# A hybrid attention and convolution layer: turning the normed latents, and spreading the input's row norm, by VectorE and DRAM in place of TensorE

## The chip, the core and the metric

The kernel runs on one core of a Trainium2 chip. The core has TensorE (matmuls, with a separate weight load for each, results in PSUM), VectorE, ScalarE, GpSimd (called POOL in the profile) and SyncE (SP), which here only issues transfers; sixteen DMA engines move data between DRAM and SBUF for all the queues. In the profile VectorE is DVE and ScalarE is ACT. The metric is the device time of one execution in microseconds, as a median over runs.

## The reference, cut to what matters

The layer takes `x` (256 tokens by 2048 features) in float32, normalises its rows, and projects it with one wide `w_in` to ten pieces. The change touches the path of the first three pieces: the query latent, the key-value latent (512 features each) and the rotary key (64).

```python
def _rmsnorm(x, g):
    r = lax.rsqrt(jnp.mean(xf * xf, axis=-1, keepdims=True) + RMS_EPS)
    return (xf * r * g).astype(x.dtype)

h = _rmsnorm(x, pre_norm_g)
proj = jnp.einsum('bsd,de->bse', h, w_in)
(q_a, c_kv, k_rope, z_mla, c_in, b_gate, c_gate, z_conv, g_mla, g_conv) = jnp.split(proj, cuts, axis=-1)
q  = jnp.einsum('bsr,re->bse', _rmsnorm(q_a, q_a_norm_g), w_q_b)
kv = jnp.einsum('bsr,re->bse', _rmsnorm(c_kv, kv_a_norm_g), w_kv_b)
...
k_rope = _apply_rope(k_rope, cos, sin)
attn = _causal_mla_attention(q_nope, q_rope, k_nope, k_rope, v)
attn = attn * jax.nn.silu(z_mla)
...
x = x + _rmsnorm(out, post_norm_g)
```

Sixteen heads of attention follow, a gated short convolution beside it, two output projections with sigmoid gates, and one more projection with a norm.

## The kernel before, in words

**Precision.** Each float32 operand of a large matmul is kept as a high part and a low part, both in the fp32r type, and a product is three matmuls: high by high, high by low, low by high (`product`, L221). The high part is a copy on ScalarE and the low part a subtraction on VectorE (`split_act`, L236, for the weights; the same two engines with a scale for `x`, in `split_scaled`, L334).

**Layout.** `x_both` holds `x` with features on the partitions, times the norm's gain. The row factor of the input's norm is not applied to it: it is a number per token, `r_col` (tokens on partitions) or `r_x` (a row of 256 that stands on all partitions), and it multiplies results later.

**Weights.** All weight pieces stand in one list (`plan`, L106), in the order in which TensorE uses them: the query latent's pieces (these carry `x` too), the key-value latent's four, the rotary key's, then per head the gate's, the group's and the convolution's. `load_raw` (L150) issues them on SP's queue into three `raw` buffers; `split_unit` (L162) splits each half of a piece into `whi` and `wlo`, of which there are five each. `ahead` (L196) is called at each use and traces loads up to three pieces ahead and splits one piece ahead. A load waits until the splits of the piece three before it are done; a split waits until TensorE has finished the half that had its slot.

**Order.** The program is traced in the order of the code, and a planner that simulates the core's timeline then chooses the order on each engine among what is ready. `keep_in_program_order` pins an instruction behind the last one traced before it on its engine. Matmuls are pinned, and so are the transfers of `turned` on GpSimd's queue and the table work on GpSimd; weight loads, weight splits and most other work are not. On each engine and queue the chosen order is then kept: an instruction that waits holds up those behind it.

**The stage of the change.** The loops at L495 and L501 compute the two latents with tokens on partitions (`latent_products`, L456). After the second `ckv` piece the input's row norm is computed (`input_norm`, L361) and the query latent is normed (`latent_norm`, L465): squares on ScalarE, a power on GpSimd, a scaled copy from PSUM to `lat_f` in SBUF. The rotary key `kr` follows (L514), then `input_rows` (L374): two float32 matmuls of a matrix of ones with the diagonal matrices `dg` put the row factors on all partitions, and ScalarE copies them to `r_x`. Then the key-value latent is normed.

The next products need the latents with features on the partitions. `latent_turn` (L477) does that with eight TensorE transposes against the identity `ident` for each latent, into two PSUM banks, and from there ScalarE and VectorE make the high and low parts in `qa` and `ckv` with the norm's gain as the scale. It is called in the first gate (`gates`, L663; `z` in the profile): for `qa` after its first quarter, for `ckv` inside its second. Then come `key_rope` (L523) after the third quarter, `gates_done` (L668: sigmoid on ScalarE, product on VectorE), and the first head's groups: `qn` and `kn` (L545), `qr` (L554) and `vv` (L567), then the convolution's products `cv` and the scores `sc` (L582).

Elsewhere the kernel turns blocks another way: `turned` (L308) transposes 32x32 blocks on VectorE into a buffer `via`, stores it to a DRAM tile `far` with four transfers that put the blocks in their places, and loads it back. It is used on GpSimd's queue for the probabilities, gates and channels.

Of the kernel before, what the change touches and what calls it, by code (L numbers as in the profile page):

```python
# [10 lines left out]

F32 = mybir.dt.float32
F32R = mybir.dt.float32r
# [5 lines left out]
P = 128  # L19
S = 256  # L20
# [62 lines left out]
def tile_layer(ctx: ExitStack, tc: tile.TileContext, xw, x, pos, pvec, post_g, wc, wz, wcv, wkr, wqk, wqr, wv, cwr, wsq, out):  # L83
    nc = tc.nc

    def matmul(*a, **kw):

        return tc.keep_in_program_order(nc.tensor.matmul(*a, **kw))  # L88

    def transpose(*a):  # L90
        return tc.keep_in_program_order(nc.tensor.transpose(*a))  # L91

    const = ctx.enter_context(tc.tile_pool(name="const", bufs=1))
    top = ctx.enter_context(tc.tile_pool(name="top", bufs=1, side="right"))
# [156 lines left out]
        o, _ = PV[name]  # L251
        return pv[:, o + k : o + k + 1]

    ident = const.tile([P, P], F32, name="ident")
    make_identity(nc, ident[:, :])
    ones = const.tile([P, P], F32, name="ones")
    nc.gpsimd.memset(ones[:, :], 1.0)
    mhalf = const.tile([P, 1], F32, name="mhalf")
# [5 lines left out]
    idle = bank("idle", tag="st", bufs=1)  # L264
    for _ in range(9):
        matmul(idle[:, :P], ones[:, :], ones[:, :], start=True, stop=True)
    const.tile([P, LINE - 8 + 112], F32, name="const_pad")
    cos_t = const.tile([P, S], F32, name="cos_t")
    sin_t = const.tile([P, S], F32, name="sin_t")
    r_x = const.tile([P, S], F32, name="r_x")  # L270
# [29 lines left out]
    def temp(name, shape=(P, S), dt=F32, bufs=2, tag=None):  # L300

        tag, n = tag or name.rstrip("0123456789_"), shape[-1]
        if n % LINE == 0:
            return bp.tile(list(shape), dt, name=name, tag=tag, bufs=bufs)
        return bp.tile([P, -(-n // LINE) * LINE], dt, name=name, tag=tag, bufs=bufs)[:, :n]


    def turned(src, via, n):  # L308

        via = via[:, : P * n]  # L310
        v = via.rearrange("p (q k x) -> p q k x", q=4, k=n)
        nc.vector.transpose(v.rearrange("p q k x -> p k q x"), src)  # L312
        far = dram.tile([P, P * n], F32, name="far", tag=f"far{n}", bufs=4)

        def go():
            f = far[:, :].rearrange("(q y) (i m) -> i y q m", q=4, i=4)
            for i in range(4):
                m = via[32 * i : 32 * i + 32, :].rearrange("y (q m) -> y q m", q=4)
                tc.keep_in_program_order(nc.gpsimd.dma_start(out=f[i], in_=m))  # L319

        def come(dst):

            tc.keep_in_program_order(nc.gpsimd.dma_start(out=dst, in_=far[:, :]))

        return go, come

# [34 lines left out]
    def input_norm():  # L361
        ss = squares("x", [(x_tok[:, t, :], x_tok[:, t, :]) for t in range(NT)])
        v = temp("v_x", (P, NT), tag="rms_v")
        nc.vector.tensor_scalar(v[:, :], ss[:, :], 1.0 / D, EPS, op0=ALU.mult, op1=ALU.add)
        inverse_root(r_col[:, :], v[:, :])
        nc.vector.tensor_tensor(r_sq[:, :], r_col[:, :], r_col[:, :], op=ALU.mult)
        dgs = []
        for t in range(NT):
            dg = temp(f"dg{t}", (P, P), tag=f"rms_d{t}", bufs=1)
            nc.vector.tensor_scalar(dg[:, :], ident[:, :], r_col[:, t : t + 1], None, op0=ALU.mult)  # L370
            dgs.append(dg)
        return dgs

    def input_rows(dgs):  # L374

        rb = bank("rb", tag="st", bufs=1)
        for t in range(NT):
            matmul(rb[:, t * P : (t + 1) * P], ones[:, :], dgs[t][:, :], start=True, stop=True)
        nc.scalar.activation(r_x[:, :], rb[:, :S], AF.Copy)


    def whole(dst, ps):
# [82 lines left out]
    def latent_norm(name, pss):  # L465

        f = lat_f[name]
        ss = squares(name, [(pss[t][:, :], f[:, t, :]) for t in range(NT)])
        v, r = temp(f"v_{name}", (P, NT), tag="rms_v"), temp(f"r_{name}", (P, NT), tag="rms_r")
        nc.vector.scalar_tensor_tensor(v[:, :], ss[:, :], 1.0 / R, r_sq[:, :], op0=ALU.mult, op1=ALU.mult)  # L470
        nc.vector.tensor_scalar(v[:, :], v[:, :], EPS, None, op0=ALU.add)
        inverse_root(r[:, :], v[:, :])
        nc.vector.tensor_tensor(r[:, :], r[:, :], r_col[:, :], op=ALU.mult)
        for t in range(NT):
            nc.scalar.activation(f[:, t, :], pss[t][:, :], AF.Copy, scale=r[:, t : t + 1])

    def latent_turn(name, both, g, tags):  # L477
        f = lat_f[name]
        for j2 in range(2):
            ps = bank(f"lt_{name}{j2}", tag=tags[j2][0], bufs=tags[j2][1])  # L480
            for j in range(2):
                for t in range(NT):
                    o, b = j * S + t * P, 2 * j2 + j
                    transpose(ps[:, o : o + P], f[:, t, b * P : (b + 1) * P], ident[:, :])
            for j in range(2):
                b, src = 2 * j2 + j, ps[:, j * S : (j + 1) * S]
                nc.scalar.activation(both[:, b, :S], src, AF.Copy, scale=col(g, b))
                nc.vector.scalar_tensor_tensor(
                    both[:, b, S:], src, col(g, b), both[:, b, :S].bitcast(F32), op0=ALU.mult, op1=ALU.subtract
                )  # L490

    table_parts = tables()
    next(table_parts)
# [7 lines left out]
    for i in range(4):  # L501
        w = take(u_ckv[i])
        for k4 in range(4):
            latent_products(ps_c, 4 * i + k4, w, k4)
        if i == 0:
            next(table_parts)
        if i == 1:
            dg = input_norm()
            latent_norm("qa", ps_q)
            next(table_parts)  # L510
    ahead(u_kr)
    w = splits.pop(u_kr)
    ps = bank("kr")
    for k in range(KD):  # L514
        matmul(ps[:, :], w[k // 8][:, k % 8], x_both[:, k, :], start=k == 0, stop=k == KD - 1)
    input_rows(dg)
    latent_norm("ckv", ps_c)
    whole(kr_f, ps)
    nc.vector.tensor_copy(kr_g[:DR, :], kr_f[DR:, :])
    nc.vector.tensor_copy(kr_g[DR:, :], kr_f[:DR, :])  # L520
# [129 lines left out]
    at_t = at_f[:, :, :].rearrange("p (v t k) s -> p v t (k s)", v=NV, t=NT)  # L650
    z_ps = {}

    def quarter(pss, w, i, between=None):

        for t in range(NT):
            if t and between:
                between()
            for k4 in range(4):
                k = 4 * i + k4
                a = [x_both[:, k, o + t * P : o + (t + 1) * P] for o in (0, S)]  # L660
                product(pss[t][:, :], a, w(k4, 512), k == 0, k == KD - 1)

    def gates(v, i, between=None):  # L663
        if i == 0:
            z_ps["now"] = [bank(f"z{v}_{t}") for t in range(NT)]
        quarter(z_ps["now"], take(u_gate[v][i]), i, between)

    def gates_done(v):  # L668
        for t in range(NT):
# [92 lines left out]
    for h in range(H):  # L762
        v, at = divmod(h, HV)

        if at == 0:
            for i in range(4):
                if v == 0 and i == 1:

                    def turn_keys():
                        latent_turn("ckv", ckv, "kv_g", (("mm", 4), ("mm", 4)))  # L770
                        next(table_parts)

                    gates(v, i, turn_keys)
                else:
                    gates(v, i)
                if v == 0 and i == 0:
                    latent_turn("qa", qa, "q_g", (("st", 1), ("o", 1)))
                elif v == 0 and i == 2:
                    key_rope()
                elif v and i == 0:  # L780
                    arrive()
                elif v and i == 1:
                    pt = turn(ps_by_head.pop(h - 1))
                    next(tap)
                elif v and i == 2:
                    values(h - 1, pt)
                    make("v", v)
            if v:
                next(tap)
            gates_done(v)  # L790
        if h == 0:
            for i in first:
                make(*i)
            channels(h, 0)
        if h < H - 1:
            score(h)
        if h:
            channels(h, 0)
        if at == 0:
            coming.append(gates_turn(v, 0))  # L800
        channels(h, 1)
        if at == 0:
            arrive()
            coming.append(gates_turn(v, 1))
        else:
            pt = turn(ps_by_head.pop(h - 1))
        if h == H - 2:
            score(h + 1)

        if at == 2 or h == H - 1:  # L810
            next(tap)
        if at and h < H - 1:
            arrive()
        channels(h, 2)
        if at:
            values(h - 1, pt)
        else:
            arrive()
            if v:
                coming.append(channels_join(v - 1, 0))  # L820
        for i in made[h]:
            make(*i)
        if h == H - 1:
            pt = turn(ps_by_head.pop(h))
        channels(h, 3)
        if at == 2 or h == H - 1:
            next(tap)
        while coming and h < H - 1:
            arrive()
        if h == H - 1:  # L830
            values(h, pt)
        if at == 3:
            coming.append(channels_join(v, 1))
        if at == 1:
            tap = taps(v, 1)
            next(tap)
        elif at == 3 and h + 1 < H or h == H - 2:
            tap = taps(v, 0)
            next(tap)
# [244 lines left out]
```

## Time and profile before

| | |
|---|---|
| median of 3 runs | 1038.01 us (1038.0 to 1038.07) |
| the profiled execution | 1039.19 us, its span 1037.4 us |
| TensorE busy | 1027.2 us, 99% of the span |
| VectorE, ScalarE, GpSimd busy | 682.3, 526.6, 181.0 us |
| transfers | 231.04 MB, mean 223 GB/s |
| granted TensorE clock | 0.998 |

All times below are in microseconds from the start of the span unless marked ns. A row of a timeline has the start, the length, the engine, the line of the kernel, the operation, and the tiles as output<-inputs with their shapes; in brackets stands how long the engine stood idle before it and what ended that. A "q" behind an engine's name means its instruction queue, where transfers are issued. Matmuls are pipelined: their records overlap, so a row's length is not what an instruction adds to the time.

### The profile page before, as it was taken

To read this page: it belongs to the slowest core of one execution; us is meant where nothing else is said; L and a number is where in the kernel's file an instruction comes from. 1 tells how busy PE (TensorE), PEld (TensorE's weight loads), DVE (VectorE), ACT (ScalarE), POOL (GpSimd) and SP (SyncE) were. 2 spreads that over 40 slices of the span, in tenths; PEclk is the share of its full clock that TensorE was granted. 3 is DMA by queue.
4 is the path that set the end of the run, shared out by engine and by line. 5 is a ranking of instruction groups with operands and counts; after the bars stand their busy time and mean duration, and the time that the engine had idled before them with its cause. 6 is when DMAs were issued, how large, how long until landed. Compare 5 with 4: busy or idle time off the path is not lost.

```text
span 1037.4 us, 12723 instructions
## 1 busy us (share of the span) xinstructions
PE 1027.2 (99%) x4694; PEld 856.3 (83%) x4694; DVE 682.3 (66%) x954; ACT 526.6 (51%) x733; POOL 181.0 (17%) x345
## 2 busy tenths in 40 slices
PE   9999999999999999999999999999999999999996
PEld 7888888888888888888888888888888888888885
DVE  7579777787687786767777785564465455455562
ACT  7767555555555455554554564444334434443551
POOL 7620321114211232212313120020010001002000
PEclk9999999999999999999999999999999999999999
DMA  8745766568565685757676766565555566558642
GB/s 323 304 175 215 232 213 234 193 222 295 190 250 202 219 282 189 272 210 243 236 262 200 261 228 212 183 228 198 203 203 209 197 203 236 181 191 331 235 165 82
DMA packets 41952, 231.04 MB, mean 223 GB/s; under 512 B 7521, under 2 KB 8225, under 8 KB 18977
## 3 DMA queue, kind: packets, MB, share of 16 engines
q1 hardware_dynamic: 29808, 197.54, 53.9%
q0 software_dynamic: 11648, 29.38, 8.5%
q10 hardware_dynamic: 432, 3.29, 0.8%
q8 instruction: 37, 0.61, 0.2%
q14 instruction: 27, 0.21, 0.1%
HBM read 214.48 MB, written 11.53 MB: 218 GB/s over the span
## 4 chain that ended last, share of the span: by engine, by line
PE 98%; DMA 1%; DVE 0%; ACT 0%; SPq 0%; DVEq 0%; issue 0%
PE cv L88 34%; PE sq L88 34%; PE z L88 8%; PE out L88 8%; PE qn L88 2%; PE kn L88 2%; PE vv L88 2%; PE ckv L88 2%; PE qa L88 2%; PE sc L88 1%; PE qr L88 1%; PE o L88 1%; DMA raw<-xw_dram 1%; PE kr L88 0%; DVE og L971 0%; PE lt_qa L91 0%
## 5 line engine op out<-in xcount | busy, mean ns | idle before, releaser
L238 DVE TENSOR_TENSOR wlo<-raw,whi 128x1024 fp32r<-128x1024 f32 (+1 forms) x370 | 441.1, 1198 | 284.1 <-ACT whi L237 273.9
L237 ACT ACTIVATE whi<-raw 128x1024 fp32r<-128x1024 f32 (+1 forms) x372 | 382.9, 1035 | 396.2 <-PE sq L88 180.5
L88 PE MATMUL cv<-whi,x_both 128*128 128x512 f32 x1024 | 321.1, 389 | 0.0
L88 PEld LDWEIGHTS cv<-whi,x_both 128*128 128x128 f32 x1024 | 192.3, 188 | 39.2
L88 PE MATMUL cv<-wlo,x_both 128*128 128x512 f32 x512 | 199.5, 390 | 0.0
L88 PE MATMUL sq<-whi,x_both 128*128 128x512 f32 x512 | 158.3, 389 | 0.0
L88 PEld LDWEIGHTS sq<-whi,x_both 128*128 128x128 f32 x512 | 96.1, 188 | 19.9
L88 PEld LDWEIGHTS cv<-wlo,x_both 128*128 128x128 f32 x512 | 96.2, 188 | 19.0
L88 PE MATMUL sq<-wlo,x_both 128*128 128x512 f32 x256 | 99.6, 389 | 0.0
L88 PE MATMUL z<-whi,x_both 128*128 128x512 f32 x256 | 80.6, 390 | 0.0
L88 PE MATMUL sq<-whi,at_both 128*128 128x512 f32 x256 | 79.5, 389 | 0.0
L88 PE MATMUL sq<-whi,cv_both 128*128 128x512 f32 x256 | 79.4, 389 | 0.0
L88 PE MATMUL out<-whi,m_both 128*128 128x512 f32 x256 | 78.9, 389 | 0.0
L319 POOL DMA_DIRECT2D far<-sg x32 | 17.5, 555 | 312.2 <-DVE sg L312 238.6
L319 POOL DMA_DIRECT2D far<-via x64 | 35.4, 560 | 195.1 <-DVE via L312 194.7
L88 PEld LDWEIGHTS sq<-wlo,x_both 128*128 128x128 f32 x256 | 48.0, 188 | 10.0
L88 PEld LDWEIGHTS z<-whi,x_both 128*128 128x128 f32 x256 | 48.1, 188 | 9.9
L88 PEld LDWEIGHTS sq<-whi,at_both 128*128 128x128 f32 x256 | 48.0, 188 | 9.9
L88 PEld LDWEIGHTS out<-whi,m_both 128*128 128x128 f32 x256 | 48.0, 188 | 9.9
L88 PEld LDWEIGHTS sq<-whi,cv_both 128*128 128x128 f32 x256 | 48.0, 188 | 9.9
L88 PE MATMUL z<-wlo,x_both 128*128 128x512 f32 x128 | 49.8, 389 | 0.0
L88 PE MATMUL sq<-wlo,at_both 128*128 128x512 f32 x128 | 49.8, 389 | 0.0
(214 smaller groups left out, 1128.0 us busy)
## 6 DMA issues: line engine op xcount, KB each, us to landing
raw<-wsq_dram SPq DMA_DIRECT2D x80, 1024.0 KB, 4.7
raw<-wcv_dram SPq DMA_DIRECT2D x64, 1024.0 KB, 5.8
raw<-wz_dram SPq DMA_DIRECT2D x16, 1024.0 KB, 4.7
raw<-wqk_dram SPq DMA_DIRECT2D x8, 1024.0 KB, 5.1
cw<-cwr_dram POOLq DMA_DIRECT2D x24, 256.0 KB, 6.2
raw<-wc_dram SPq DMA_DIRECT2D x4, 1024.0 KB, 9.9
raw<-wv_dram SPq DMA_DIRECT2D x4, 1024.0 KB, 4.7
far<-via POOLq DMA_DIRECT2D x64, 48.0 KB, 3.3
```

The lines of the kernel that those rows point to most:

```text
L88: return tc.keep_in_program_order(nc.tensor.matmul(*a, **kw))
L237: a = nc.scalar.activation(hi, src, AF.Copy)
L238: b = nc.vector.tensor_tensor(lo, src, hi.bitcast(F32), op=ALU.subtract)
L319: tc.keep_in_program_order(nc.gpsimd.dma_start(out=f[i], in_=m))
```

## The change

`ident`, `transpose`, `input_rows` and `latent_turn` go. The input's norm stores `r_col` to a DRAM row and loads it back on all partitions (`r_come`). `turned` takes a queue and a DRAM destination, and `latent_norm` uses it on SP's queue, that of the weights: per latent two VectorE transposes and eight stores, and later one load (`qa_come`, `ckv_come`) back to where the normed latent stood. `latent_split` then makes the high and low parts from SBUF. The calls move: `qa` is split after the gate's third quarter, `ckv` after its fourth, and the key's rope comes after the second. Pads keep the SBUF places of the other tiles.

```diff
-    ident = const.tile([P, P], F32, name="ident")
-    make_identity(nc, ident[:, :])
...
-    def turned(src, via, n):
+    def turned(src, via, n, queue=nc.gpsimd, far=None):
...
-        far = dram.tile([P, P * n], F32, name="far", tag=f"far{n}", bufs=4)
+        if far is None:
+            far = dram.tile([P, P * n], F32, name="far", tag=f"far{n}", bufs=4)[:, :]
         def go():
-            f = far[:, :].rearrange("(q y) (i m) -> i y q m", q=4, i=4)
+            f = far.rearrange("(q y) (i m) -> i y q m", q=4, i=4)
             for i in range(4):
                 m = via[32 * i : 32 * i + 32, :].rearrange("y (q m) -> y q m", q=4)
-                tc.keep_in_program_order(nc.gpsimd.dma_start(out=f[i], in_=m))
+                tc.keep_in_program_order(queue.dma_start(out=f[i], in_=m))
...
     def input_norm():
...
-        dgs = []
-        for t in range(NT):
-            dg = temp(f"dg{t}", (P, P), tag=f"rms_d{t}", bufs=1)
-            nc.vector.tensor_scalar(dg[:, :], ident[:, :], r_col[:, t : t + 1], None, op0=ALU.mult)
-            dgs.append(dg)
-        return dgs
-    def input_rows(dgs):
-        rb = bank("rb", tag="st", bufs=1)
-        for t in range(NT):
-            matmul(rb[:, t * P : (t + 1) * P], ones[:, :], dgs[t][:, :], start=True, stop=True)
-        nc.scalar.activation(r_x[:, :], rb[:, :S], AF.Copy)
+        temp("pad_n", (P, S), bufs=1)
+        far = dram.tile([1, S], F32, name="far_r")
+        tc.keep_in_program_order(nc.sync.dma_start(out=far[:, :].rearrange("o (t p) -> p (o t)", t=NT), in_=r_col[:, :]))
+        return lambda: tc.keep_in_program_order(nc.sync.dma_start(out=r_x[:, :], in_=far[:, :].to_broadcast([P, S])))
...
+        far = dram.tile([P, NT * R], F32, name=f"far_{name}")
         for t in range(NT):
             nc.scalar.activation(f[:, t, :], pss[t][:, :], AF.Copy, scale=r[:, t : t + 1])
-    def latent_turn(name, both, g, tags):
-        f = lat_f[name]
-        for j2 in range(2):
-            ps = bank(f"lt_{name}{j2}", tag=tags[j2][0], bufs=tags[j2][1])
...
+            go, _ = turned(f[:, t, :], temp("cw", (P, 512), bufs=2), 4, nc.sync, far[:, t * R : (t + 1) * R])
+            go()
+        return lambda: tc.keep_in_program_order(
+            nc.sync.dma_start(out=f, in_=far[:, :].rearrange("p (t c) -> p t c", t=NT))
+        )
+    def latent_split(name, both, g):
+        f = lat_f[name].rearrange("p t (i k x) -> p k t i x", i=4, k=KR)
+        for k in range(KR):
+            hi, lo = (both[:, k, o : o + S].rearrange("p (t i x) -> p t i x", t=NT, i=4) for o in (0, S))
+            tc.keep_in_program_order(nc.scalar.activation(hi, f[:, k], AF.Copy, scale=col(g, k)))
+            tc.keep_in_program_order(
+                nc.vector.scalar_tensor_tensor(lo, f[:, k], col(g, k), hi.bitcast(F32), op0=ALU.mult, op1=ALU.subtract)
+            )
...
         if i == 1:
-            dg = input_norm()
-            latent_norm("qa", ps_q)
+            r_come = input_norm()
+            qa_come = latent_norm("qa", ps_q)
             next(table_parts)
+        if i == 3:
+            r_come()
+            qa_come()
...
-    input_rows(dg)
-    latent_norm("ckv", ps_c)
+    ckv_come = latent_norm("ckv", ps_c)
...
-                if v == 0 and i == 1:
-                    def turn_keys():
-                        latent_turn("ckv", ckv, "kv_g", (("mm", 4), ("mm", 4)))
-                        next(table_parts)
-                    gates(v, i, turn_keys)
-                else:
-                    gates(v, i)
+                gates(v, i)
                 if v == 0 and i == 0:
-                    latent_turn("qa", qa, "q_g", (("st", 1), ("o", 1)))
+                    ckv_come()
+                elif v == 0 and i == 1:
+                    next(table_parts)
+                    key_rope()
                 elif v == 0 and i == 2:
-                    key_rope()
+                    latent_split("qa", qa, "q_g")
...
             if v:
                 next(tap)
+            else:
+                latent_split("ckv", ckv, "kv_g")
             gates_done(v)
```

More of the change, by code (lines that the diff above doesn't have):

```diff
@@ L9 @@
 from concourse._compat import with_exitstack
-from concourse.masks import make_causal_mask, make_identity
+from concourse.masks import make_causal_mask
 F32 = mybir.dt.float32
@@ L88, in matmul @@
         return tc.keep_in_program_order(nc.tensor.matmul(*a, **kw))
-    def transpose(*a):
-        return tc.keep_in_program_order(nc.tensor.transpose(*a))
     const = ctx.enter_context(tc.tile_pool(name="const", bufs=1))
@@ L266, in tile_layer @@
         matmul(idle[:, :P], ones[:, :], ones[:, :], start=True, stop=True)
-    const.tile([P, LINE - 8 + 112], F32, name="const_pad")
+    const.tile([P, LINE - 8 + 112 + P], F32, name="const_pad")
     cos_t = const.tile([P, S], F32, name="cos_t")
@@ L312, in turned @@
         nc.vector.transpose(v.rearrange("p q k x -> p k q x"), src)
-        far = dram.tile([P, P * n], F32, name="far", tag=f"far{n}", bufs=4)
+        if far is None:
+            far = dram.tile([P, P * n], F32, name="far", tag=f"far{n}", bufs=4)[:, :]
         def go():
-            f = far[:, :].rearrange("(q y) (i m) -> i y q m", q=4, i=4)
+            f = far.rearrange("(q y) (i m) -> i y q m", q=4, i=4)
             for i in range(4):
                 m = via[32 * i : 32 * i + 32, :].rearrange("y (q m) -> y q m", q=4)
-                tc.keep_in_program_order(nc.gpsimd.dma_start(out=f[i], in_=m))
+                tc.keep_in_program_order(queue.dma_start(out=f[i], in_=m))
         def come(dst):
-            tc.keep_in_program_order(nc.gpsimd.dma_start(out=dst, in_=far[:, :]))
+            tc.keep_in_program_order(queue.dma_start(out=dst, in_=far))
         return go, come
@@ L473, in latent_norm @@
         nc.vector.tensor_tensor(r[:, :], r[:, :], r_col[:, :], op=ALU.mult)
+        far = dram.tile([P, NT * R], F32, name=f"far_{name}")
         for t in range(NT):
             nc.scalar.activation(f[:, t, :], pss[t][:, :], AF.Copy, scale=r[:, t : t + 1])
-    def latent_turn(name, both, g, tags):
-        f = lat_f[name]
-        for j2 in range(2):
-            ps = bank(f"lt_{name}{j2}", tag=tags[j2][0], bufs=tags[j2][1])
[L481 to L490, printed above, removed]
+            go, _ = turned(f[:, t, :], temp("cw", (P, 512), bufs=2), 4, nc.sync, far[:, t * R : (t + 1) * R])
[11 more added lines that the diff above has]
+            )
     table_parts = tables()
@@ L651, in tile_layer, with quarter @@
     z_ps = {}
-    def quarter(pss, w, i, between=None):
+    def quarter(pss, w, i):
         for t in range(NT):
-            if t and between:
-                between()
             for k4 in range(4):
@@ L661, in quarter, with gates @@
                 product(pss[t][:, :], a, w(k4, 512), k == 0, k == KD - 1)
-    def gates(v, i, between=None):
+    def gates(v, i):
         if i == 0:
             z_ps["now"] = [bank(f"z{v}_{t}") for t in range(NT)]
-        quarter(z_ps["now"], take(u_gate[v][i]), i, between)
+        quarter(z_ps["now"], take(u_gate[v][i]), i)
     def gates_done(v):
```

## The prediction

> **What bounds the kernel now.** I read the page's busy times first, then the chain of work that ended last, then that chain in order of time, and only after that the tiles that the change touches. The first three say that TensorE is the bound almost everywhere.
>
> ```profile
> span 1037.4 us, 12723 instructions
> PE 1027.2 (99%) x4694; PEld 856.3 (83%) x4694; DVE 682.3 (66%) x954; ACT 526.6 (51%) x733; POOL 181.0 (17%) x345
> PE 98%; DMA 1%; DVE 0%; ACT 0%; SPq 0%; DVEq 0%; issue 0%
> ...
> 1.64 6.58 DMA raw<-xw_dram
> 9.33 19.38 PE qa L88 x84
> ...
> 50.47 3.63 PE kr L88 x16
> 54.54 5.46 PE z L88 x24
> 60.87 2.75 PE z L88 x12
> 64.49 13.64 PE z L88 x60
> 78.13 2.77 PE qn L88 x16
> 80.90 2.79 PE kn L88 x16
> ...
> 594.38 348.20 PE sq L88 x1536
> ```
>
> The columns of the chain are start, length, engine, product, line and count. The reader is to see that the chain goes from TensorE to TensorE, so what is taken off TensorE comes off the end, and work on the other engines is free until TensorE waits for it. The pace of a wide matmul follows from the last row: 348.20 / 1536 = 0.2267 us. With it the holes can be measured. From the start of `kr` (50.47) to the start of `qn` (78.13) pass 27.66 us; the rows between hold 16 + 24 + 12 + 60 = 112 matmuls, worth 112 x 0.2267 = 25.39 us. The other 2.27 us are what the change takes away: 0.44 between `kr` and `z` (54.54 - 54.10), 0.87 between 60.00 and 60.87, 0.87 between 63.62 and 64.49, and 0.09 of slower neighbours.
>
> The view of those tiles says what stands in the holes.
>
> ```profile
> L88 PE MATMUL rb<-dg,ones x4: 270/274/275, 53.9 to 54.3; 128*128 128x128 f32 x4
> L91 PE MATMUL lt_qa<-ident,at_f x8: 270/272/273, 59.8 to 60.6; 128*128 128x128 f32 x8
> ...
> L91 PE MATMUL lt_ckv<-ident,at_f x8: 272/273/273, 63.5 to 64.2; 128*128 128x128 f32 x8
> ```
>
> **TensorE's term: -2.27 us.** The change drops 16 transposes and the four records of the two `rb` matmuls, and puts nothing in their place on TensorE. Duration times count would give 20 x 0.272 = 5.4 us, but these instructions overlap; the holes in the chain are the price, so I take 2.27.
>
> [...]
>
> **The start: 0.** `ident` costs POOL a memset and a select ahead of the warm-up matmuls, but the chain starts with the load of `xw` and `qa` gets going at 9.33 behind it. That load is neither moved nor delayed. The bounds are 0 and the little by which POOL is done sooner, and the load hides it.
>
> **The input's row norm: 0.** A store of 1 KB in 4-byte pieces and a broadcast load replace two `dg` operations on VectorE, `rb`, and a ScalarE copy. The nearest rows stand below: 8 KB in 6.1 us on POOL's queue, and the quickest, 128 KB in 2.0 on SP's; two in a row are 4.0 to 12.2 us.
>
> ```profile
> ta_i<-pos_dram POOLq DMA_DIRECT2D x4, 8.0 KB, 6.1
> far<-cw POOLq DMA_DIRECT2D x48, 64.0 KB, 4.9
> out_dram<-og SPq DMA_DIRECT2D x4, 128.0 KB, 2.0
> raw<-wqr_dram SPq DMA_DIRECT2D x8, 256.0 KB, 2.6
> raw<-wkr_dram SPq DMA_DIRECT2D x1, 512.0 KB, 7.7
> raw<-wz_dram SPq DMA_DIRECT2D x16, 1024.0 KB, 4.7
> 41.49 0.16 DVE L366 TENSOR_TENSOR r_both<-r_both 128x2 f32<-128x2 f32 x1 [0.84 <-POOL r_both L358]
> 58.63 0.43 DVE L389 TENSOR_TENSOR at_f<-at_f,r_x 128x256 f32<-128x256 f32 x1
> ```
>
> (In the transfers: issuing queue, count, size, us from issue to landing.) `r_col` stands at 41.49 and its row is first used at 58.63, so even 12.2 us fit into the 17.1. If that cover went, only the key's rope would be late, and what needs it are the scores, far behind (their row comes below).
>
> **The latents' turn.** Each latent now takes two VectorE transposes, eight stores and one load on SP's queue, then four ScalarE and four VectorE splits. The splits are the old ones moved. `ckv` is the tight one, because its norm waits for POOL.
>
> ```profile
> 45.58 1.25 ACT L475 ACTIVATE at_f<-qa,r_qa 128x512 f32<-128x512 f32 x2
> 57.83 0.69 POOL L358 TENSOR_TENSOR r_ckv<-v_ckv,mhalf 128x2 f32<-128x2 f32 x1
> 58.80 1.27 ACT L475 ACTIVATE at_f<-ckv,r_ckv 128x512 f32<-128x512 f32 x2 [3.07 <-DVE r_ckv L473]
> L312 DVE STREAM_TRANSPOSE cw<-at_f 128x512 f32<-128x512 f32 x8 | 5.6, 703 | 0.0
> L319 POOL DMA_DIRECT2D far<-via x64 | 35.4, 560 | 195.1 <-DVE via L312 194.7
> L237 ACT ACTIVATE kr<-at_f 128x256 fp32r<-128x256 f32 x1 | 0.4, 397 | 0.0
> 55.04 0.33 SPq L157 DMA_DIRECT2D raw<-wqk_dram  x1
> 62.30 0.33 SPq L157 DMA_DIRECT2D raw<-wqr_dram  x1
> ```
>
> For `qa` there is time: its norm is done at 45.58 + 1.25 = 46.8, its products start at 78.13, and TensorE has `ckv`, `kr` and `z` to do meanwhile. POOL's table copies hold `r_ckv`, not TensorE, so this start does not move. The normed `ckv` is whole at 60.07, the second transpose ends at 60.07 + 0.70 = 60.8, and the first set of stores can go at 60.3. Eight issues at SP's 0.33 end at 63.0, at POOL's 0.56 at 64.8. A store lands between 2.0 (SP's row) and 4.9 us (POOL's, the same size and shape) after its issue; the load takes 2.6 to 7.7 us, and by its size of 512 KB lies between the rows of 256 KB and 1 MB, about 3.3. The quick sum is 63.0 + 2.0 + 0.33 + 3.3 = 68.6, the slow one 64.8 + 4.9 + 0.33 + 7.7 = 77.7. SP's own rows are nearer, and the 512 KB row stood behind other loads, so I take 70.
>
> [...]
>
> When is it due? Before the run of work that follows it on ScalarE and VectorE.
>
> ```profile
> 71.43 1.06 ACT L237 ACTIVATE whi<-raw 128x1024 fp32r<-128x1024 f32 x1 [3.02 <-PE z L88]
> 75.50 1.28 ACT L671 ACT_TABLE_LOAD   x1 [2.08 <-PE z L88]
> 77.51 0.75 DVE L672 SCALAR_TENSOR_TENSOR at_f<-z,r_both,at_f 128x512 f32<-128x512 f32 x1 [2.83 <-ACT at_f L671]
> 94.92 0.87 DVE L238 TENSOR_TENSOR qr<-f,qr 64x256 fp32r<-64x256 f32 x2
> 96.03 0.34 PE L88 MATMUL sc<-kr,qr 128*128 128x256 f32 x1
> ...
> 60.00:66.00 6.00, 6.00 (x36) 5.16 (x35) 4.80 (x8) 4.64 (x10) 0.00 (x0) 1.00 0.15 44
> 66.00:72.00 6.00, 6.00 (x28) 4.98 (x27) 5.60 (x11) 2.98 (x5) 0.00 (x0) 1.00 0.24 68
> 72.00:78.00 6.00, 6.00 (x29) 4.95 (x28) 2.65 (x4) 3.90 (x6) 0.00 (x0) 1.00 0.76 289
> 87.00:90.00 3.00, 3.00 (x15) 2.47 (x14) 2.99 (x7) 1.81 (x4) 0.00 (x0) 1.00 0.18 68
> ```
>
> The split of `ckv` is pinned on ScalarE behind the second half of `wqk` (71.43 before, 69.2 when TensorE is 2.27 early) and in the code stands ahead of the gate's sigmoid, whose table load moves from 75.50 to 73.2. Four splits of 0.40 are 1.6 us, so data that land by 73.2 - 1.6 = 71.6 cost nothing: 1.6 us to spare at an arrival of 70. VectorE has air in the same stretch (windows: length, then busy time of PE, PEld, DVE, ACT, POOL): between 60 and 78 it is busy 4.80 + 5.60 + 2.65 = 13.05 of 18 us. Take 1.83 us of room away (the part of the 2.27 that falls here) and add two transposes of 0.70: 4.95 - 1.83 - 1.41 = 1.7 us are left. From 77.51 on it has none (2.99 busy of 3.00 in the stretch shown), until the low half of `qr` at 95.79, 0.24 us ahead of the score matmul at 96.03 that reads it. So lateness above these margins reaches TensorE at the first scores, less 0.24.
>
> The loads behind the new waits: SP stands at the stores from about 60 to 63 and again until the load can go, near 66. The weights next in line were issued at 55.04 (`wqk`, used at 78.13) and 62.30 (`wqr`, whose products come after `kn`, past 80.90 + 2.79 = 83.7). Held back 4 us, 62.30 becomes 66.3 and lands at 68.9: no one waits. For `qa` the stores fall between 47 and 52, and what may stand behind them is a load of `wz`; the last 24 `z` matmuls start at 78.13 - 24 x 0.2267 = 72.7, some 20 us later. I take 0 for SP, with the price in the rivals if `wqk` is what stands behind.
>
> **Sum.** Against the profiled execution, 1039.19 us with 1037.4 of span: -2.27 + 0 + 0 + 0 = 1036.9. The median of the runs shown is 1038.01, 1.18 below that execution, so the same sum there is 1035.7; I name 1035.8 for small change in the order.
>
> **The rivals.**
> *Part of it is given back.* The arrival comes at 72 to 74, or VectorE's 1.7 us are not where they are needed, and the first scores wait 0.3 to 2.2 us: 1036.0 to 1038.0, middle 1037. For it speaks the saturated run with 0.24 us at its end, and that POOL's stores took 4.9; against it, that SP's queue is nearly idle from 60 to 72 (a DMA share of 0.15 and 0.24 in the windows).
> *ScalarE stands at the split of `ckv`.* With the slow end, 77.7, the split ends 77.7 - 71.6 = 6.1 us late, the sigmoid, VectorE's run and the scores with it: 1035.7 + 6.1 - 0.24 = 1041.6. The point of balance is an arrival at 71.6 + 0.24 + 2.27 = 74.1, and 0.2% slower is reached at 76.2. If `wqk` waits behind the `ckv` load, it goes at 66.6, lands at 73 and its two halves and the split (3.7 us) end at 76.7 in place of 73.2, which alone gives 1039. Against it: `wqk` was ready at 55.04, five microseconds before the first store of `ckv`.
> *The holes close but TensorE waits for something else in the same place,* the weights of `z` above all: 1038.0. Against it: the chain shows no step but TensorE there, and the splits of `z` end before their products begin.
>
> [...]
>
> **How the numbers follow.** 0.2%, here 2.1 us, is about what a measurement of this kernel can tell from no change, and the whole gain is 2.27, so a loss of 0.2 us already makes it "the same". I give the clean case 0.54 (1035.3 to 1036.0), part given back 0.25, no gain 0.05, ScalarE's wait 0.16. That makes 0.54 faster, 0.30 same, 0.16 slower. The range from 1035.3 to 1038.3 holds the first three cases.
>
> **What would show it.** Right: in the chain `z` follows `kr` at once and 96 `z` matmuls run in 21.8 us; `qn` starts near 75.9; the load of `ckv` lands by 71.6; the sigmoid's table load stands near 73.2; the first scores near 93.8 without a gap. Wrong: a hole on TensorE between 75 and 96, an ACT idle put down to the load of `at_f`, or a weight load on SP issued several us after its slot was free and a TensorE wait behind it.

## The result, and the profile after

The changed kernel takes 1043.46 us (median of 6 runs, 1042.86 to 1043.8) against 1038.04 for the kernel before in runs beside it (6 runs, 1037.86 to 1038.38): a ratio of 1.005, 95% interval 1.004 to 1.0061. It is 5.4 us slower where 2.2 us of gain had been forecast. The profiled execution took 1042.86 us, the least of its six; that of before (1039.19) stood 1.15 above its median, so the two spans, 1041.1 and 1037.4, differ by only 3.7.

The page's busy times, its chain by engine, and the rows of the chain in order of time (start, length, step) that answer to those of before:

```profile
span 1041.1 us, 12720 instructions
PE 1027.6 (99%) x4674; PEld 856.0 (82%) x4674; DVE 684.5 (66%) x956; ACT 526.6 (51%) x732; POOL 176.7 (17%) x343
...
PE 97%; DVE 1%; DMA 1%; ACT 0%; issue 0%; DVEq 0%; POOL 0%; ACTq 0%; POOLq 0%
...
27.79 10.33 PE ckv L88 x46
...
49.07 7.78 DMA raw<-wz_dram
...
56.93 1.06 ACT whi L234
...
58.02 2.36 DVE wlo L235 x2
60.38 0.35 DVE at_f L374
...
60.77 21.23 PE z L88 x84
81.99 2.77 PE qn L88 x16
...
598.24 21.80 PE sq L88 x96
```

The chain no longer goes from TensorE to TensorE. It leaves at a load of `wz`, the gate's weights, and comes back at 60.77. Everything lies in one place: from `qn` to `sq` it is 594.38 - 78.13 = 516.25 us before and 598.24 - 81.99 = 516.25 after, while from the start of `ckv` to `qn` it is 78.13 - 28.71 = 49.42 before and 81.99 - 27.79 = 54.20 after, 4.8 more. Had the 2.27 us of holes merely closed, it would be 47.15; so 7.05 us were lost in the stretch.

What SP issued in that stretch, and what TensorE, ScalarE and VectorE did (start, length, engine, line, instruction; in brackets the idle time before it and what ended that):

```profile
41.05 0.38 SPq L366 DMA_DIRECT2D far_r<-r_both  x1
48.63 0.34 SPq L367 DMA_DIRECT2D r_x<-far_r  x1
49.07 0.85 SPq L154 DMA_DIRECT2D raw<-wz_dram  x2
49.97 9.70 SPq L315 DMA_DIRECT2D far_qa<-cw  x8
...
55.51 0.39 PE L88 MATMUL z<-whi,x_both 128*128 128x512 f32 x1
60.77 0.79 PE L88 MATMUL z<-whi,x_both 128*128 128x512 f32 x1 [4.87 <-DVE at_f L374]
...
56.93 2.00 ACT L234 ACTIVATE whi<-raw 128x1024 fp32r<-128x1024 f32 x2 [6.30 <-DMA raw<-wz_dram]
58.84 0.36 ACT L373 ACTIVATE half<-kr 128x256 f32<-128x256 f32 x1
...
60.30 0.42 DVE L374 TENSOR_TENSOR at_f<-kr,half 128x256 f32<-128x256 f32 x1
```

Read it from below. `z` needs the PSUM bank in which the rotary key `kr` stood. The key is taken out by ScalarE (58.84) and VectorE (60.30). ScalarE has the split of the second `wz` piece ahead of that in its order, and stood 6.30 us because the piece had not landed. Its load was issued at 49.07, with the next piece's behind it, and in the kernel before at 45.08 (in the same view of before, where one row holds three loads):

```profile
45.08 5.04 SPq L157 DMA_DIRECT2D raw<-wz_dram  x3
```

The load stood on SP behind that of `r_x`, which had to wait until the 1 KB store of the norm's row had landed; that took 7.6 us. And once issued it took 7.78 us to land, against 4.7 for this kind of load before (the median of sixteen). The windows (length; busy time of PE, PEld, DVE, ACT, POOL; granted clock, DMA share, GB/s) show two more things:

```profile
47.00:50.00 3.00, 3.00 (x15) 2.49 (x14) 2.40 (x4) 1.18 (x4) 2.83 (x10) 1.00 0.02 5
50.00:53.00 3.00, 3.00 (x15) 2.48 (x14) 0.37 (x2) 0.63 (x3) 2.71 (x14) 1.00 0.68 50
56.00:60.70 4.70, 0.00 (x0) 0.00 (x0) 2.68 (x3) 3.33 (x4) 0.00 (x0) 0.71 0.89 323
60.70:64.50 3.80, 3.73 (x9) 2.96 (x10) 3.69 (x10) 1.41 (x3) 0.00 (x0) 0.50 0.88 326
```

From 50 to 53 the transfer engines are 0.68 busy and move 50 GB/s. The same window of the kernel before has 1.03 and 344:

```profile
50.00:53.00 3.00, 3.00 (x15) 2.48 (x14) 0.80 (x3) 2.72 (x6) 2.71 (x14) 1.00 1.03 344
```

And after the hole the granted clock is 0.50, so that nine `z` matmuls fill 3.8 us. Of the 7.2 us lost between the start of `z` (53.02) and `qn` (28.97 us for 96 matmuls, worth 21.76), the hole is 60.77 - 55.74 = 5.0 and the slow matmuls 21.23 - 84 x 0.2267 = 2.2.

### The profile page after: what moved, and what is told of

Read it like the earlier page. It is cut to its first block, busy times and chain, and to the rows that moved or that the text cites. A ratio compares the mean times of both kernels' runs of the same rounds, so it can differ in the third digit from the quotient of the medians.

```text
span 1041.1 us, 12720 instructions
## 1 busy us (share of the span) xinstructions
PE 1027.6 (99%) x4674; PEld 856.0 (82%) x4674; DVE 684.5 (66%) x956; ACT 526.6 (51%) x732; POOL 176.7 (17%) x343
## 4 chain that ended last, share of the span: by engine, by line
PE 97%; DVE 1%; DMA 1%; ACT 0%; issue 0%; DVEq 0%; POOL 0%; ACTq 0%; POOLq 0%
PE cv L88 34%; PE sq L88 33%; PE out L88 8%; PE z L88 8%; PE qa L88 2%; PE qn L88 2%; PE kn L88 2%; PE vv L88 2%; PE sc L88 1%; PE qr L88 1%; PE ckv L88 1%; PE o L88 1%; DMA raw<-wz_dram 1%; DVE wlo L235 1%; PE idle L88 0%
```

## The experiments

Two causes stood against each other in the first expectations. One, called S, is the order on SP: the load of `r_x` waits on the queue ahead of the weights. The other, called T, is the eight stores of `qa` on that queue, or their traffic. A third, called U, was named only when these two had been tried: that the store of 256 pieces of 4 bytes is itself what slows the transfers around it, whoever waits.

**The row's load later on SP.**

```diff
         if i == 3:
-            r_come()
             qa_come()
...
                 if v == 0 and i == 0:
+                    r_come()
                     ckv_come()
```

> The change with one call moved: the load of the row factor (r_come) is traced after the first gate quarter, so that on SP's queue the second and third load of wz stand ahead of it. Theory S (SP stands still at the row factor's load, waiting for the 4-byte store, and the wz loads behind it come late): the second wz load is issued near 45 us again, the 5 us hole in z and the slow matmuls after it are gone, and the time is 1036 us, 2 below the kernel before. Rival T (the eight stores of qa on the queue, or their traffic, make the weights late): the hole stays, 1041 to 1044 us.

Measured: 1041.56 us, ratio 1.0033 (1.0021 to 1.0045). SP's view, the chain, TensorE's waits (what it waited for: us in all, times, the longest) and the windows:

```profile
44.99 1.61 SPq L154 DMA_DIRECT2D raw<-wz_dram  x2
...
44.99 11.06 DMA raw<-wz_dram
...
PE z L88 <- DVE at_f L374: 4.1, 1, 4.1
...
47.00:50.00 3.00, 3.00 (x15) 2.48 (x14) 2.74 (x4) 1.19 (x4) 2.88 (x8) 1.00 0.50 27
```

The `wz` load is now issued at its old time and takes 11.06 us. S as the whole cause falls: the load is late although nothing held it on SP, while the engines are half busy and move 27 GB/s. The time lies in the range named for T, but T is not shown by that; the next two runs speak on it.

**Each half of the change alone.** The row through DRAM alone, in the kernel before (the latents still turned by TensorE); and the latents' turn alone, in the changed kernel (the row again by `dg` and `rb`):

```diff
 # the row alone, in the kernel before
-            dg = input_norm()
+            r_come = input_norm()
...
+        if i == 3:
+            r_come()
...
-    input_rows(dg)

 # the turn alone, in the kernel after
-            r_come = input_norm()
+            dg = input_norm()
...
-            r_come()
             qa_come()
...
+    input_rows(dg)
```

> The kernel before with only the input's row norm sent through DRAM on SP's queue; the latents are still turned on TensorE. Theory S: rb goes (-0.44 us), but the second wz load waits behind the row factor's load, z waits some 5 us for its PSUM bank and then runs slowly for 2: 1042 to 1045 us. Rival T: no hole without the latents' stores, 1037.6 us.

> The change with the input's row norm put back on TensorE (ident, dg, rb and the copy to r_x); the latents go by VectorE and DRAM on SP's queue as in the change. Theory S: no hole, and the transposes' holes of 1.83 us are saved: 1036.2 us. Rival T: hole stays, 1041 to 1044 us.

Measured: the row alone 1046.4 us (5 runs, 1043.85 to 1046.74), ratio 1.0071 (1.0059 to 1.0084), 1.4 us above the expected range; the turn alone 1036.18 us, ratio 0.9981 (0.9972 to 0.999). The chain and waits of the row alone:

```profile
50.15 8.56 DMA raw<-wz_dram
...
62.63 4.84 PE z L88 x12
...
PE z L88 <- DVE at_f L377: 6.7, 1, 6.7
```

and the chain of the turn alone:

```profile
28.00 21.76 PE ckv L88 x96
...
53.83 21.77 PE z L88 x96
75.60 2.77 PE qn L88 x16
```

T falls: the row alone has the hole without those stores, and the turn alone has the stores and no hole. All of the loss is the row's, and the turn gains 1.9 us by itself. From `ckv` to `qn` it takes 75.60 - 28.00 = 47.60, 1.82 less than before. The ratios 1.005 and 0.9981 put the row's price at 0.0069 x 1038 = 7.2 us, what the trace after had lost in its stretch.

**Another bank for the key.** If the bank of `kr` were the cause and not only the place where lateness shows, `z` would run on with another one.

```diff
-    ps = bank("kr")
+    ps = bank("kr", tag="cv", bufs=2)
```

> The change with the rotary key's PSUM bank taken from the two cv banks, not from the four that z uses. The load order on SP is left as it is. Theory S with the bank as the link (the key's evacuation on ScalarE stands behind the split of the late wz piece, and z's second token block waits for its bank): z no longer waits for the bank but for the late weights themselves, which by the changed kernel's trace are split at 58 to 59 us where TensorE wants them at 58.5: a hole under 1.5 us and no slow matmuls, 1036 to 1038 us. Rival B (the weights alone are what z waits for): the hole of 5 us stays, 1043 us.

Measured: 1043.15 us, ratio 1.0044 (1.0031 to 1.0057), no gain that can be told from the changed kernel. TensorE's waits:

```profile
PE z L88 <- ACT whi L234: 1.5, 1, 1.5
PE kn L88 <- DVE at_f L661: 1.3, 1, 1.3
...
PE z L88 <- DVE wlo L235: 0.8, 1, 0.8
```

The expectation missed: the time is that of rival B, though the one hole of 5 us has become three short ones, and the clock falls here too (0.59 on average from 62 to 66). The wait on the bank is gone, and the same late weights are waited for directly, at their split and later at the gate's end. The bank was the place, not the cause.

**The row in pieces of 128 bytes.** VectorE first transposes `r_both` in 32x32 blocks, and four stores write the row in eight pieces of 128 bytes. The load follows at the same place.

```diff
+    nc.gpsimd.memset(r_both[:, :], 0.0)
...
-        temp("pad_n", (P, S), bufs=1)
+        rt = temp("pad_n", (P, S), bufs=1)[:, :LINE]
+        nc.vector.transpose(rt, r_both[:, :])
...
-        tc.keep_in_program_order(nc.sync.dma_start(out=far[:, :].rearrange("o (t p) -> p (o t)", t=NT), in_=r_col[:, :]))
+        f = far[:, :].rearrange("o (t q x) -> q (o t) x", t=NT, q=4)
+        for q in range(4):
+            tc.keep_in_program_order(nc.sync.dma_start(out=f[q], in_=rt[32 * q : 32 * q + NT, :]))
```

> The change with the row factor turned on VectorE first (one 32x32 transpose of r_both, which is zeroed at the start), so that the row goes to DRAM in 8 pieces of 128 B by four stores in place of 256 pieces of 4 B by one; the broadcast load stays, and SP waits for it at the same place. Theory U (the 4-byte pieces themselves hold the transfers up for some 8 us): the store lands in 2 to 3 us, the second wz load lands by 51, no hole: 1035.8 us, a little under the kernel with the latents' turn alone. Rival V (the wait on SP's queue or the broadcast load does it): a hole stays, 1040 us and more.

Measured: 1036.14 us (11 runs, 1035.33 to 1036.43), ratio 0.9981 (0.9972 to 0.999). SP's view, the chain, and ScalarE's split of `ckv`:

```profile
42.02 1.20 SPq L370 DMA_DIRECT2D far_r<-pad_n  x4
44.09 0.35 SPq L371 DMA_DIRECT2D r_x<-far_r  x1
45.16 1.62 SPq L154 DMA_DIRECT2D raw<-wz_dram  x2
...
28.11 21.76 PE ckv L88 x96
...
53.50 21.76 PE z L88 x96
75.26 2.77 PE qn L88 x16
...
69.87 1.71 ACT L480 ACTIVATE ckv<-at_f,pv 128x256 fp32r<-128x256 f32 x4 [0.26 <-DMA at_f<-far_ckv]
```

The same row by the same way, in other pieces: the load of `r_x` goes at 44.09 in place of 48.63, the weights at 45.16, and there is no hole. From `ckv` to `qn` it is 47.15, the 49.42 of before less 2.27. This version does all that the change does and is 0.2% faster than the kernel before, as the turn alone is (1036.18); the 0.44 us of `rb` between these two is in the traces and not in the medians.

**A store that nobody reads.** The turn alone, with a store of `r_col` to DRAM whose row is never loaded, so that nothing waits for it. Six forms of it: packed at 4 bytes on SP's queue; its pieces 512, 64 and 16 bytes apart; packed on GpSimd's queue; and half of it, 128 packed pieces.

```diff
+        far = dram.tile([1, S], F32, name="far_r")
+        tc.keep_in_program_order(nc.sync.dma_start(out=far[:, :].rearrange("o (t p) -> p (o t)", t=NT), in_=r_col[:, :]))
 # on GpSimd's queue: nc.gpsimd in place of nc.sync; half: [1, P], t=1 and r_col[:, :1]
 # 512 bytes apart (64 and 16 with 16 and 4 in place of P in the tile)
+        far = dram.tile([S, P], F32, name="far_r")
+        tc.keep_in_program_order(nc.sync.dma_start(out=far[:, :].rearrange("(t p) w -> p t w", t=NT)[:, :, 0], in_=r_col[:, :]))
```

> The kernel with the latents' turn alone (row norm on TensorE) and beside it the 4-byte store of the row factor on SP's queue, which nobody reads or waits for. Theory U: the store alone makes the second wz load some 8 us slower, z gets its hole: 1040 to 1042 us. Rival V: 1036.2 us as without it.

> As the kernel with the dead store, but the 256 pieces of 4 B go to places 512 B apart in DRAM. If they are slow because they fall together in 1 KB (U1): the store lands in 2 to 3 us and the time is 1036.2 us. If each piece has its price wherever it goes (U2): as the dead store, 1040 to 1042 us.

> As the kernel with the dead store, but issued on POOL's queue; SP's queue holds the wz loads alone. If the hold-up is in SP's own queue, behind the store in order (U3): 1036.2 us, with the store as slow as before. If it is in the engines or in DRAM, which all queues share (U4): the wz load is late again, 1040 to 1042 us.

> The kernel with the latents' turn and the dead store, its 256 pieces of 4 B now 64 B apart (16 KB in all). If what hurts is several pieces within 64 B: the store lands in 2 us, TensorE has no hole, 1036 us. If it is pieces within a longer stretch of DRAM (512 B was free): the store takes 4 to 9 us, 1037 to 1042 us.

> The turn alone with the unread store again, its 4-byte pieces 16 B apart, so that four of them lie in the same 64 B and none touches the next. If what hurts is that several pieces fall into the same 64 B, the store is still slow (landing clearly over the 1.6 us of the wide pitches, between 3 and 9 us) and the time lies between 1037 and 1041 according to it. If what hurts is that the pieces are contiguous (packed at 4 B), it lands in 1.6 us as at 64 B and the time is 1036.

> The turn alone with an unread store of half as many pieces, 128 of 4 B, packed into 512 B. If each packed piece has its price, worked out from the full store (9.0 us to land against 1.6 spread, so 7.4 / 256 = 0.029 us a piece), it lands 1.6 + 3.7 = 5.3 us after its issue, the second load of z's weights is late by about 1.2 us of the 4.9 seen, and the time lies between 1036 and 1038. If the price belongs to the packed store whatever its length, it lands in about 9 us and the time is 1040 to 1041.

| store | time, us | ratio (95%) | store lands in | second `wz` load lands in |
|---|---|---|---|---|
| none (the turn alone) | 1036.18 | 0.9981 (0.9972 to 0.999) | | 4.8 us |
| packed, SP | 1040.81 | 1.0033 (1.0019 to 1.0046) | 9.0 us | 10.46 |
| packed, GpSimd's queue | 1041.26 | 1.0033 (1.0022 to 1.0044) | 9.9 | 10.82 |
| half of it, packed, SP | 1040.49, one run | | 8.4 | 9.67 |
| 16 bytes apart, SP | 1036.11, one run | | 1.6 | 4.8 |
| 64 bytes apart, SP | 1035.87, one run | | 1.6 | 4.8 |
| 512 bytes apart, SP | 1036.15 | 0.9983 (0.9974 to 0.9992) | 1.6 | 4.7 |

The rows behind it, first of the packed store on SP (transfers, chain, windows), then of that on GpSimd's queue, that 16 bytes apart, and the half (transfers, and TensorE's waits):

```profile
far_r<-r_both SPq DMA_DIRECT2D x1, 1.0 KB, 9.0
...
44.38 10.46 DMA raw<-wz_dram
...
47.00:50.00 3.00, 3.00 (x15) 2.49 (x14) 2.13 (x3) 1.18 (x4) 2.79 (x10) 1.00 0.62 35
```

```profile
far_r<-r_both POOLq DMA_DIRECT2D x1, 1.0 KB, 9.9
...
45.30 10.82 DMA raw<-wz_dram
```

```profile
far_r<-r_both SPq DMA_DIRECT2D x1, 1.0 KB, 1.6
...
53.41 21.78 PE z L88 x96
```

```profile
far_r<-r_both SPq DMA_DIRECT2D x1, 0.5 KB, 8.4
...
PE z L88 <- DVE at_f L387: 2.3, 1, 2.3
```

A packed store that no instruction waits for costs (1.0033 - 0.9981) x 1038 = 5.4 us by the ratios, and 1040.81 - 1036.18 = 4.6 by the medians. That is most of the row's 7.2; the other 1.8, by the ratios, are what SP's wait for the row can have added, though the intervals of the changed kernel and of the later load (1.004 to 1.0061, 1.0021 to 1.0045) overlap, so that part is not shown. The queue is no part of it: from GpSimd's queue the store does the same to SP's loads, with 10.82 us for the second `wz` load against 10.46 from SP's own. Nor is it the number or the size of the pieces as the program writes them, which is the same in five of the six. It is not the number of packets either: the trace has the packed store as 256 packets of 4 bytes on SP's queue and as 16 of 64 bytes on GpSimd's, and both are slow.

The trace's own records of single packets, counted by the us in which they start, say where the time goes. With the packed store on SP:

```
start, us   4-byte packets       8192-byte packets
40          -                    50, mean 309 ns each
41 to 42    288, 9 ns each       33, mean 309 ns (all before 42)
43 to 44    -                    -
45          -                    14, mean 3874 ns, up to 6341
46          -                    2, mean 6373 ns
47          -                    1, 1433 ns
48          -                    7, mean 2181 ns
49          -                    5, mean 2599 ns
50          -                    3, mean 1691 ns
51          -                    4, mean 811 ns
52          -                    46, mean 310 ns
```

Of the 288 small packets 256 are the store's pieces. All are gone through by 43, at 9 ns each. The store is still reported as landed only at about 50, and the weights' packets that start between 45 and 52 take up to some twenty times their 309 ns. With the pieces 16 bytes apart the 49 packets that start in the us from 46 take 309 ns.

In two of these runs the first of the two theories fell and the second came. For 16 bytes apart the first had four pieces in the same 64 bytes as enough to be slow, and the store was quick; the limit lies between a step of 16 and one of 4 bytes. The step also sets the stretch of DRAM, 4 KB at 16 bytes and 1 KB packed, and no run tells the one from the other. For the half the first had a price for each piece; half the pieces took 8.4 us, nearly as long as all. What holds a packed store so long stays open.

**The clock behind the hole.** To tell the hole's own price from that of the clock after it, 22 matmuls of ones (44 records) fill it, in the changed kernel.

```diff
         for t in range(NT):
+            if t and between:
+                between()
...
+                def fill():
+                    busy = bank("busy", tag="st", bufs=1)
+                    for _ in range(22):
+                        matmul(busy[:, :P], ones[:, :], ones[:, :], start=True, stop=True)
+                gates(v, i, fill if v == 0 and i == 0 else None)
```

> The change with 22 float32 128x128 matmuls of ones (some 5 us of them at full clock, result unused) put between the two token blocks of the first gate quarter, where the changed kernel's TensorE stands idle for 5 us and then runs at half the granted clock for some 4. If the slow stretch comes from the idleness (theory C): the hole is filled, the late block starts at the same time, the granted clock stays 1.00 after it, and about 1.9 us come back: 1041.5 us. If the slow stretch has another cause (weights that come slowly): 1043.4 us, or up to 5 more if the fillers push z.

Measured: 1042.43 us, ratio 1.0047 (1.0029 to 1.0065). The chain, TensorE's fillers, and the window that had 0.50:

```profile
62.56 19.35 PE z L88 x84
...
55.75 5.07 PE L88 MATMUL busy<-ones 128*128 128x128 f32 x44
...
60.70:64.50 3.80, 2.06 (x10) 1.61 (x9) 3.72 (x7) 1.35 (x3) 0.00 (x0) 1.00 0.79 226
```

The clock stays at 1.00 and the same 84 matmuls take 19.35 us in place of 21.23, so 1.9 us of the loss in that trace were the clock's. The time is between the two that were expected, 1041.5 and 1043.4: the hole itself ended 1.8 us later in this execution (the store landed in 8.9 us, not 7.6), and of the gain 1.0 is seen in the medians, inside their intervals.

## Why the prediction was wrong, and where it was right

*TensorE's term, -2.27 us:* right. With the row in pieces of 128 bytes the stretch from `ckv` to `qn` is 47.15 us against 49.42; with the turn alone it is 1.82 less, the 2.27 without the 0.44 of `rb`. The times, 1036.14 and 1036.18, are 0.3 to 0.4 above the 1035.8 forecast.

*The start, 0:* `ckv` starts between 27.3 and 28.7 in the traces, with and without the change; nothing of it can be put down to `ident`.

*The latents' turn:* right. Arrival was forecast at 70 and due at 71.6. With the row in pieces of 128 bytes the stores of `ckv` went from 60.48 on, the load at 65.74, and ScalarE began the split at 69.87 after 0.26 us of idle time; the first scores run without a gap. The stores held SP longer than eight issues of 0.33 us (3.7 us for `ckv`, 6.0 for `qa` in the turn alone), and nothing waited for that. In the changed kernel the eight of `qa` took 9.70, from 49.97 on, where the windows show the transfers held up (50 GB/s from 50 to 53).

*The input's row norm, 0:* this is the step that failed. It set the latency of a store and a load, 4.0 to 12.2 us, against the 17.1 us until `r_x` is used, and the row came in time: store issued at 41.05, load landed near 54.3. That is 13.3 us, above the upper bound of 12.2, because the store alone took 7.6 where 6.1 was the most allowed; the cover of 17.1 was wide enough all the same. But it asked only who reads the row. It did not ask what stands behind the waiting load on SP, although the three `wz` loads were there in the trace of before, from 45.08 on, and a store of 2.0 to 6.1 us, its own bounds, after 41.49 ends at 43.5 to 47.6, beside them. That alone is not what cost most. The larger part, 5.4 us, is that the store slows the transfers beside it (in the turn alone with the unread store on SP the second `wz` load took 10.46 us in place of 4.8), and no row of before shows a store of packed 4-byte pieces; the rows taken as its nearest were a load of 8 KB and a store of 128 KB. The bounds were for the row's own two transfers; for what they do to the others the sum had no term.

*The rivals.* That TensorE waits in the same place, "the weights of `z` above all", is what came, at a chance of 0.05 and a price of 1038.0. It named the place and no cause for it. The price was wrong: it took the hole as at most the old holes' 2.27 us, and it was 5.0 with 2.2 of slow clock behind it. The objection to it, that `z`'s splits end before its products begin, describes loads that come on time. ScalarE did stand, as the slower rival had it, but at a weight and not at `ckv`. Of the signs of a wrong forecast the last one came as written: a weight load on SP issued several us late and a TensorE wait behind it.

*Holes or durations.* The sum took the holes in the chain, 2.27 us, and not the durations times the count, 20 x 0.272 = 5.4. With all twenty records gone (the row in pieces of 128 bytes) the stretch from `ckv` to `qn` is shorter by 2.27: the holes were the right price.

## What to carry to other kernels

Price a small transfer by its pieces in DRAM and by what it does to the transfers beside it, not by its own latency against its reader: a column of one number per partition, written packed into a row, cost 5.4 us here though nobody read it, and a 32x32 transpose ahead of the store, which makes pieces of 128 bytes, made it free (1036.14 us against 1036.18 for the turn alone). When a load that waits for a store is put on the weights' queue, list what that queue issues next and who waits for it. A wait that TensorE shows names the last link (here a PSUM bank); follow it back through the engines that work in order, and test the first link by removing it.

## What the hardware showed that was not expected

Two hundred and fifty-six 4-byte pieces packed into 1 KB of DRAM took 7.6 to 9.9 us to land in every kernel that had them, and a 1 MB load issued 3.6 to 4.0 us behind them took 10.46 to 11.06 in place of 4.7 to 4.8, on the same queue or on another; half as many, packed, took 8.4 and the load behind them 9.67; 16 bytes apart all 256 took 1.6.

How long TensorE stands does not settle by itself what its clock does. Behind holes of 4.1 us (the later load), 4.9 (the changed kernel) and 6.7 (the row alone) the granted clock was 0.50 for 5.9, 4.0 and 4.0 us; behind 2.8 (packed, SP) and 3.4 (packed, GpSimd's queue) it stayed at 1.00; but behind two short holes of 1.5 and 0.8 (the key's other bank) it fell too, and so it did behind the 2.3 of the half store:

```profile
60.00:61.00 1.00, 1.00 (x3) 0.77 (x3) 0.97 (x4) 0.11 (x1) 0.00 (x0) 0.50 0.79 311
```

In the changed kernel the clock fell within the hole: the window from 56.00 to 60.70 has a mean of 0.71, which puts the fall from 1.00 to 0.50 near 58.0, some 2.2 us into the hole that began at 55.74. What else decides it stays open.
